# Splitting the last phase's weights ahead, handing the projection buffers over as rings, and a shrinking lead in the last unit of a streaming encoder layer

## The chip, the core and the metric

One core of a Trainium2 chip runs the whole layer as one program. The metric is the device time of one execution in microseconds (us), from the runs listed below. The core's engines work in parallel, each in the order of its own queue: PE (TensorE, matrix products and transposes; its weight loads are listed apart as PEld), DVE (VectorE), ACT (ScalarE), POOL (GpSimd), and SP, which issues the DMA transfers. They wait for each other through semaphores.

## What is computed

One layer over 2048 prompt rows (16 tiles of 128) and 8 x 16 sample rows (one more tile, called NT), model width 1024. Cut to its core:

```python
def adaln_modulate(x, c, norm_g, w_ada, b_ada):
    shift, scale, gate = jnp.split(c @ w_ada + b_ada, 3, axis=-1)
    return rms_norm(x, norm_g) * (1.0 + scale[:, None, :]) + shift[:, None, :], gate[:, None, :]

# qa ka va za (4 heads of 2 x 64), qb kb vb zb (8 heads of 64), gates ga gb: one product
qa, ka, va, za, qb, kb, vb, zb, ga, gb = jnp.split(h @ w_in, idx, axis=-1)   # rope on qa, ka

# a: softmax pair, mask by chunks of 64     w = p[0] - lam * p[1]
# b: stick breaking, mask kpos < qpos       log_a = log_sigmoid(z) + (suffix sum of log_sigmoid(-z))
oa, ob = diff_attention(qa, ka, va), stick_breaking_attention(qb, kb, vb)

oa = rms_norm(oa, subln_g) * (1.0 - lam_init)
ya = (oa * silu(za)) @ w_branch_a
yb = (ob * silu(zb)) @ w_branch_b
y  = x + gate * ((sigmoid(ga) * ya + sigmoid(gb) * yb) @ w_out)
return rms_norm(y, final_g)          # and the new keys and values
```

The sample rows attend to a cache of 512 positions per stream as well. Everything is float32 in and out; the products are made in pairs of float16 numbers.

## The kernel before

**Split numbers.** A float32 operand is scaled and written as a float16 high part and a float16 rest (`split`, L266: the high part on ACT, POOL or DVE, the rest on DVE by one scalar_tensor_tensor at L274). A product is then three float16 products. The scale comes from the sum of squares of the whole operand (`sum_squares` L246, `scales` L212), so weights are read once for their norm and once more to be cut.

**Phases.** First, adaLN and the modulated rows, written split to DRAM (`hT_d`). Then eight *units*, one for each of the four a-heads and four pairs of b-heads in turn (kind 0 and 1). A unit projects each of the 17 tiles (24 matmuls of 512 columns, L409), makes a slice of the gates for it as well (L476; none in the first unit, 512 columns wide in the last, 256 in the others), and runs attention for the 16 prompt tiles: scores (L611, L612), for kind 1 two sigmoids, a scan on DVE (L588) and a product on POOL (L594), then a cast and a subtraction (L544, L545), a DMA transpose (`wt`, L552), and two steps later the products with the values (`pv`, L663, L664). Results go to DRAM (`o_d`, `z_d`, `g_d`). The *last phase* reads them for each tile: `inputs` (L1105) normalises, applies silu and splits to u16, transposes it to uT; `branches` (L1218) multiplies by the branch weights `wb`, merges by the gates, splits to y16 and transposes to yT; `output` (L1253) multiplies by `wo` and writes the row. The sample's attention over the cache runs beside it, as 55 lists of pieces (`lane`, L1287) dealt to the tiles' iterations by `aside`.

**What sets the order.** The main loop (L1162) goes through the 136 steps (unit, tile). At each it takes pieces from one long line of projection pieces up to a target position and interleaves them with the step's scores and the products of two steps before. The target is the share of the attention time passed, plus `LEAD`, 5 tiles: projection stays five tiles ahead of attention. *Spare* work, one piece at a time, fills in after the next unit's weights are ready (L1174): 80 pieces that only sum squares, of the 16 slices of the branch and output weights and of 64 slices of the caches. When the line is at its end, `early_work` gives the freed projection memory to the last phase: it cuts the branch weights (8 pieces) and makes the inputs of the first two tiles. A scheduler then sorts the instructions of each engine by a model of readiness, so the order in which they are written is a wish.

**Memory.** The projection's buffers are pools on the right side: 12 pieces of split weights (`wpr`), two staging tiles (`wst`), three tiles of rows (`hst`, tag hg), six gate weights (`gw`) and two gate results (`gt`). `proj.close()` frees them all; then wb (4 MB), the inputs' tiles (`inp`) and a stage for cutting are opened there. The output weights are cut at the start of the last phase, in memory freed by attention (L1205), through two tiles that the output rows use later.

## Time and profile before

| | us |
|---|---|
| median of three runs | 2507.16 (2504.18 to 2513.22) |
| the profiled execution | 2508.37 |
| its span, first to last instruction | 2506.5 |
| last gate matmul of the units starts | 1850.44 |
| last product of attention with values starts | 1925.69 |
| first branch matmul starts | 1933.03 |
| first output matmul starts | 1960.8 |
| mean granted TensorE clock | 0.940 |

In a row of the page's instruction groups stand: line, engine, operation, output and inputs by the program's names (buffer numbers left out), shapes and count, then busy time and mean duration in ns, then the idle time of the engine before them and what ended it. In a row of waits: who waited for what, total us, times, longest. In a timeline row: start, duration, engine, line, and in brackets the idle time before and its releaser. The 40 digits of a slice row are tenths of the time that the engine was busy, for TensorE's clock (PEclk) tenths of full speed. A matmul's duration includes its passage through the array, so that neighbours overlap; the distance between starts is its price.

### The profile page before, as it was taken

The numbers are of one execution on the slowest core, as the hardware profiler recorded it, in microseconds if no ns is written. First come the engines' busy times: TensorE is split into PE (matmuls) and PEld (weight loads), VectorE is DVE, ScalarE is ACT, GpSimd is POOL, SyncE is SP. The second block draws the span as 40 slices with busy tenths as digits, with TensorE's granted clock in tenths as the row PEclk, the third lists the DMA queues.
The fourth block names the chain that finished last, engine by engine and source line by source line (L and its number), as shares of the span: only waits on it lengthen the run. The fifth ranks groups of instructions, "written<-read, shape, count | busy, mean of one in ns | idle before, by whom it ended". The sixth has DMA issues, their size and how long they took to land. (4 is left out here: it accounts for less than half of the span.)

```text
span 2506.5 us, 45283 instructions
## 1 busy us (share of the span) xinstructions
PE 2195.5 (88%) x16366; PEld 1275.3 (51%) x16366; DVE 1793.3 (72%) x3762; ACT 1602.7 (64%) x3200; POOL 827.6 (33%) x671
## 2 busy tenths in 40 slices
PE   7859898899999988889989888999975788889997
PEld 3435555455655555556655555555543344444443
DVE  3577846877676678757577876656787888888765
ACT  2558757787767688657678876656775545445542
POOL 1543113354211244311034442102344454544422
PEclk8979999999999999999999999999985799899999
DMA  9578878998787899767679976656678989888531
GB/s 287 183 221 206 211 175 200 196 220 191 180 193 185 198 222 212 172 152 183 157 192 194 219 190 177 160 132 142 153 168 206 257 224 242 242 212 229 167 111 51
DMA packets 890994, 477.07 MB, mean 190 GB/s; under 512 B 540074, under 2 KB 842330, under 8 KB 890256
## 3 DMA queue, kind: packets, MB, share of 16 engines
q1 hardware_dynamic: 890768, 474.17, 76.6%
q8 instruction: 128, 2.10, 0.4%
q14 instruction: 98, 0.80, 0.1%
HBM read 272.94 MB, written 73.44 MB: 138 GB/s over the span
## 5 line engine op out<-in xcount | busy, mean ns | idle before, releaser
L409 PE MATMUL ps_mm<-wpair,hg 128*128 128x512 f16 x3120 | 789.7, 388 | 58.1 <-DMA hg<-hT_d 54.4
L594 POOL TENSOR_TENSOR sc_p<-sc_p,sc_n 128x127 f32<-128x127 f32 (+7 forms) x192 | 314.0, 1639 | 807.3 <-DVE sc_n L588 796.0
L409 PEld LDWEIGHTS <-hg 128*128 128x128 f16 x3120 | 281.9, 100 | 328.9 <-DMA hg<-hT_d 62.5
L476 PE MATMUL ps_t<-gw,hg 128*128 128x256 f16 (+1 forms) x2856 | 397.6, 293 | 2.3 <-DVE qst L504 2.3
L476 PEld LDWEIGHTS <-hg 128*128 128x128 f16 x2856 | 280.4, 100 | 96.0 <-DVE qst L504 2.6
L588 DVE TENSOR_TENSOR_SCAN sc_n<-ps_s,sc_n,zero_t 128x512 f32<-128x512 f32 x192 | 245.6, 1279 | 63.4 <-ACT ps_s L121 58.2
L611 PE MATMUL ps_s<-k,qst 128*128 128x512 f16 (+3 forms) x640 | 226.5, 355 | 53.3 <-DVE sc_n L588 41.2
L545 DVE TENSOR_TENSOR sc_n<-sc_p,sc_n 128x128 f16<-128x128 f32 (+7 forms) x192 | 229.7, 1201 | 39.2 <-ACT sc_n L544 38.8
L121 ACT ACTIVATE sc_p<-ps_s,usc 128x512 f32<-128x512 f32 (+3 forms) x320 | 205.0, 641 | 47.1 <-PE ps_s L612 25.6
L612 PE MATMUL ps_s<-k,qst 128*128 128x512 f16 (+3 forms) x640 | 226.3, 356 | 0.0
L1227 PE MATMUL ps_mm<-wb,uT 128*128 128x512 f16 x816 | 206.8, 407 | 20.5 <-DVE o L1125 12.5
L121 ACT ACTIVATE ps_s<-ps_s,usc 128x512 f32<-128x512 f32 (+3 forms) x328 | 199.9, 610 | 0.0
L1266 PE MATMUL ps_o<-wo,yT 128*128 128x512 f16 x816 | 193.0, 390 | 6.9 <-ACT wo L269 2.4
L663 PE MATMUL ps_o<-v,wt 128*128 128x128 f16 x1088 | 156.5, 226 | 39.8 <-DMA wt<-sc_n 39.7
L544 ACT CAST sc_n<-sc_p 128x128 f16<-128x128 f32 (+7 forms) x192 | 154.8, 813 | 49.5 <-POOL sc_p L594 48.7
L442 POOL TENSOR_TENSOR rot<-pr,rope 128x256 f32<-128x256 f32 x68 | 59.8, 879 | 351.8 <-ACT pr L423 293.7
L251 ACT ACTIVATE junk<-wst 128x1024 f16<-128x1024 f32 x124 | 131.6, 1062 | 47.2 <-DMA wst<-in_w_in_dram 17.4
L663 PEld LDWEIGHTS <-wt 128*128 128x128 f16 x1088 | 104.0, 102 | 90.3 <-DMA wt<-sc_n 49.7
L1227 PEld LDWEIGHTS <-uT 128*128 128x128 f16 x816 | 82.7, 104 | 125.3 <-issue 50.8
L530 DVE TENSOR_SCALAR_CACHE_REDUCE sc_n<-ps_s,usc 128x512 f32<-128x512 f32 (+3 forms) x160 | 106.6, 666 | 55.2 <-PE ps_s L615 34.2
L664 PE MATMUL ps_o<-v,wt 128*128 128x64 f16 x1088 | 145.2, 198 | 0.0
L530 DVE TENSOR_SCALAR_CACHE_REDUCE sc_p<-ps_s,usc 128x512 f32<-128x512 f32 (+3 forms) x160 | 106.5, 666 | 52.6 <-PE ps_s L612 41.7
(295 smaller groups left out, 4372.9 us busy)
## 6 DMA issues: line engine op xcount, KB each, us to landing
hg<-hT_d SPq DMA_DIRECT2D x130, 512.0 KB, 4.5
wst<-in_w_in_dram SPq DMA_DIRECT2D x112, 256.0 KB, 3.8
g<-g_d SPq DMA_DIRECT2D x34, 512.0 KB, 5.8
wst<-in_w_in_dram SPq DMA_DIRECT2D x32, 512.0 KB, 4.8
out_dram<-pr SPq DMA_DIRECT2D x204, 64.0 KB, 2.3
g_d<-gt SPq DMA_DIRECT2D x102, 128.0 KB, 3.1
wide<-in_w_ada_dram SPq DMA_DIRECT2D x12, 1024.0 KB, 10.3
z_d<-pr SPq DMA_DIRECT2D x136, 64.0 KB, 1.8
```

The lines of the kernel that those rows point to most:

```text
L121: i = S.activation(**kw)
L409: T.matmul(box["p"], box["h"][:, hi, k, :], U["w"][k][:, wi, :], start=(n == 0), stop=(n == 3 * KT - 1))
L476: T.matmul(box["g"][:, 0:gw], box["h"][:, hi, k, :], U["wg"][k // per][:, k % per, wi, :], start=(j == 0), stop=(j == 3 * KT - 1))
L530: V.tensor_scalar(out=dst[:, lo : lo + n], in0=p[:, 0:n], scalar1=sc_pos, scalar2=None, op0=ALU.mult, op1=ALU.max, accum_out=job["mx"][:, ...
L545: V.tensor_tensor(out=lo, in0=src, in1=hi, op=ALU.subtract)
L588: V.tensor_tensor_scan(out=dst[:, lo : lo + n][:, ::-1], data0=src[:, 0:n][:, ::-1], data1=zero_t[:, 0:1].to_broadcast([P, n]), initial=fi ...
L594: G.tensor_tensor(out=p[:, 0:m], in0=p[:, 0:m], in1=n[:, 1 : m + 1], op=ALU.mult)
L611: T.matmul(p[:, 0:n], qst[:, c, :], kk[:, c, 0:n], start=True, stop=False)
L612: T.matmul(p[:, 0:n], qst[:, 2 + c, :], kk[:, c, 0:n], start=False, stop=not diag)
L663: T.matmul(po[:, c * P : (c + 1) * P], wt[:, wj, :], vt[:, c, :, :], start=first, stop=False)
L1227: T.matmul(pb, st["u"][:, ui * 8 + br * 4 + k, :], wb[:, br, wi, k, c], start=(n == 0), stop=(n == 11))
L1266: T.matmul(po, st["y"][:, yi * 8 + k, :], wo[:, wi, k, c], start=(n == 0), stop=(n == 3 * KT - 1))
```

## The change

In words, part by part:

- *Weights.* The 16 cuts of the branch and output weights become 16 further pieces at the end of the spare work. Each loads 512 KB, splits it into one of two `cut` tiles, and stores the result to DRAM (`w2_d`). The spare work is dealt so that it ends with the seventh unit (before, it could reach into the eighth). The last phase loads the split pieces and cuts nothing.
- *Rings.* The projection's pools become lists of tiles of 4 KB a partition that are handed round by hand (`buf`). Six w tiles hold two split weight pieces each, as many as the twelve before; gt is one tile used in halves; two `cut` tiles are new. They stay open to the end: wb lies in two tiles each of cut, wst, w and gw, loaded as these come free from 15 steps before the end; o, z and u16 of the last phase lie in the three hg tiles, the gates in the other four gw tiles, uT in two w tiles, yT in the last two w tiles (one before), and y16 in the same tile as u16 (before: a tile of its own).
- *Lead.* In the last unit the target is written anew: from 5 tiles ahead at its start, the line's end is reached at 87% of the unit's time instead of about 70%.
- *First tiles.* After the line's end, seven pieces: inputs of two tiles, the four branch halves of the first tile with its finish, and the inputs of the third tile. The last phase's loop starts at 1; the lane of 55 lists is dealt to iterations 1 to 12 instead of 0 to 12.

The diff, cut where lines only moved or follow from those shown (`branches` moved out of the last phase into the layer's body, with the buffers named above):

```diff
-W_BUFS = 12
-G_BUFS = 6
+LAST = 0.87
+RINGS = {"w": 6, "wst": 2, "gw": 6, "hg": 3, "gt": 1, "cut": 2}
...
+    w2_d = [dram.tile([P, 2, 2, 512], F16, name=f"w2_d{i}") for i in range(16)]
-    proj = ctx.enter_context(ExitStack())
-    wpr = proj.enter_context(tc.tile_pool(name="wpr", bufs=W_BUFS, side="right", reuse_waits="tile"))
-    wst = proj.enter_context(tc.tile_pool(name="wst", bufs=2, side="right", reuse_waits="tile"))
+    rings, turns = {}, {}
+    def open_rings(name, tags):
+        pool = ctx.enter_context(tc.tile_pool(name=name, bufs=1, side="right", reuse_waits="tile"))
+        for tag in tags:
+            rings[tag] = [pool.tile([P, 1024], F32, name=f"{tag}{i}") for i in range(RINGS[tag])]
+            turns[tag] = 0
+    def buf(tag, dt=F32):
+        b = rings[tag][turns[tag] % len(rings[tag])]
+        turns[tag] += 1
+        return b if dt == F32 else b.bitcast(dt)
+    open_rings("ring0", ("w", "wst"))
...
-            st = wst.tile([P, 2, 4, P], F32, tag="wst", name="wst") if keep is None else keep[:, k // 2, :, :, :]
+            st = buf("wst").rearrange("p (k j n) -> p k j n", k=2, n=P) if keep is None else keep[:, k // 2, :, :, :]
...
-            w = gwp.tile([P, gk, 2, gw], F16, tag="gw", name="gw", bufs=G_BUFS)
+            w = buf("gw", F16).rearrange("p (k f n) -> p k f n", k=gk, f=2)
...
+            pair = buf("w", F16).rearrange("p (i f n) -> p i f n", i=2, f=2)
-                w = wpr.tile([P, 2, 512], F16, tag="wpair", name="wpair")
+                w = pair[:, i, :, :]
...
-        ahead[u, t] = hst.tile([P, 2, KT, P], F16, tag="hg", name="hg")
+        ahead[u, t] = buf("hg", F16).rearrange("p (f k n) -> p f k n", f=2, n=P)
...
-                gt = gwp.tile([P, 512], F32, tag="gt", name="gt", bufs=2)
+                gt = rings["gt"][0][:, t % 2 * 512 : t % 2 * 512 + 512]
...
-            st = wst.tile([P, 2, 4, P], F32, tag="wst", name="wst").rearrange("p k j n -> p (k j n)")
+            st = buf("wst")
-        return [lambda src=src, dst=dst: one(src, dst) for src, dst in srcs]
+        def cut(i):
+            if i == 0:
+                L["s"] = [scales(total(add_up(wsums[:, lo : lo + 8], 8)), con, f"s_w{lo}") for lo in (0, 8)]
+            src, k = ((w_ba, w_bb)[i // 4], i // 2 % 2 * 2) if i < 8 else (w_out, (i - 8) // 2 * 2)
+            st = buf("wst").rearrange("p (k n) -> p k n", k=2)
+            load(out=st, in_=src[:, k : k + 2, i % 2 * 512 : i % 2 * 512 + 512])
+            w = buf("cut", F16).rearrange("p (f k n) -> p f k n", f=2, k=2)
+            split(w[:, 0, :, :], w[:, 1, :, :], st, L["s"][i // 8][:, 0:1], S if i % 2 else G)
+            load(out=w2_d[i], in_=w)
+        return [lambda src=src, dst=dst: one(src, dst) for src, dst in srcs] + [lambda i=i: cut(i) for i in range(16)]
+    L = {}
...
-    hst = proj.enter_context(tc.tile_pool(name="hst", bufs=3, side="right", reuse_waits="tile"))
-    gwp = proj.enter_context(tc.tile_pool(name="gwp", bufs=1, side="right", reuse_waits="tile"))
+    open_rings("ring1", ("gw", "hg", "gt", "cut"))
-    late_weights = {}
-    cutting = ctx.enter_context(ExitStack())
-    L = {}
-    def cut(dst, src, k, j, s, n, pool, tag, bufs):
-        st = pool.tile([P, 2, 512], F32, tag=tag, name="wst2", bufs=bufs)
-        cols = slice(j * 512, (j + 1) * 512)
-        load(out=st, in_=src[:, k : k + 2, cols])
-        split(dst[:, 0, k : k + 2, cols], dst[:, 1, k : k + 2, cols], st, s[:, 0:1], S if n % 2 else G)
+    def weight(i, b):
+        b = b.rearrange("p (f k n) -> p f k n", f=2, k=2)
+        load(out=b, in_=w2_d[i])
+        return b
...
-        inp = L["inp"]
-        o = inp.tile([P, D], F32, tag="o2", name="o2")
+        o, z = rings["hg"][0], rings["hg"][1]
-        z = inp.tile([P, D], F32, tag="z2", name="z2")
-            gs.append(inp.tile([P, 2, 512], F32, tag="g2", name="g2", bufs=4))
+            gs.append(buf("gw").rearrange("p (b n) -> p b n", b=2))
...
-        u16 = inp.tile([P, 2, D], F16, tag="u16", name="u16")
+        u16 = rings["hg"][2].bitcast(F16).rearrange("p (f n) -> p f n", f=2)
-        uT = inp.tile([P, 16, P], F16, tag="uT", name="uT", bufs=2)
+        uT = buf("w", F16).rearrange("p (k n) -> p k n", n=P)
...
+    def branches(st):
...
+                    T.matmul(pb, st["u"][:, ui * 8 + br * 4 + k, :], L["wb"][br * 4 + k // 2 * 2 + j][:, wi, k % 2, :], start=(n == 0), stop=(n == 11))
...
+            y16 = rings["hg"][2].bitcast(F16).rearrange("p (f n) -> p f n", f=2)
...
+            yT = buf("y", F16).rearrange("p (k n) -> p k n", n=P)
...
-        res = ctx.enter_context(tc.tile_pool(name="resw", bufs=1, side="right", reuse_waits="tile"))
-        L["wb"] = res.tile([P, 2, 2, 4, D], F16, name="wb")
-        L["inp"] = ctx.enter_context(tc.tile_pool(name="inp", bufs=1, side="right", reuse_waits="tile"))
-        L["s"] = [scales(total(add_up(wsums[:, lo : lo + 8], 8)), con, f"s_w{lo}") for lo in (0, 8)]
-        stage = cutting.enter_context(tc.tile_pool(name="stage", bufs=1, side="right", reuse_waits="tile"))
-        made = [lambda k=k, j=j, br=br: cut(L["wb"][:, br, :, :, :], (w_ba, w_bb)[br], k, j, L["s"][0], br + k, stage, "wst2", 1)
-                for br in range(2) for k in (0, 2) for j in range(2)]
-        return made + [lambda t=t: first(t) for t in tiles[0:2]]
+        rings["w"] = [rings["w"][(turns["w"] + i) % 6] for i in range(4)]
+        rings["gw"] = [rings["gw"][(turns["gw"] + i) % 6] for i in range(4)]
+        turns["w"] = turns["gw"] = 0
+        rings["y"], turns["y"] = rings["w"][2:4], 0
+        del rings["w"][2:4]
+        def branch(j):
+            if j == 0:
+                L["b"] = branches(states[tiles[0]])
+            L["b"][j][1]()
+        return [lambda t=t: first(t) for t in tiles[0:2]] + [lambda j=j: branch(j) for j in range(4)] + [lambda: first(tiles[2])]
...
-                for _ in spare[: -(-len(spare) // ((NT + 1 - t % NT) + 8 * (6 - min(u, 6))))]:
+                for _ in spare[: -(-len(spare) // ((NT - t % NT) + 8 * (6 - min(u, 6))))]:
-        target = position(len(steps) * past / whole + LEAD)
+        target = len(steps) * past / whole + LEAD
+        if n >= 7 * (NT + 1):
+            target = 7 * (NT + 1) + LEAD + (NT + 1 - LEAD) / LAST * (8 * past / whole - 7)
+            if n >= len(steps) - 15 and not spare and len(L.setdefault("wb", [])) < 8:
+                i = len(L["wb"])
+                L["wb"].append(weight(i, buf(("cut", "wst", "w", "gw")[i // 2], F16)))
+        target = position(target)
-                proj.close()
-    cutting.close()
...
-        wb, (s_b, s_o) = L["wb"], L["s"]
-        wo = res.tile([P, 2, KT, D], F16, name="wo")
-        for n, (k, j) in enumerate((k, j) for j in range(2) for k in range(0, KT, 2)):
-            cut(wo, w_out, k, j, s_o, n, s2, "x", 2)
+        wo = [weight(8 + i, res.tile([P, 2048], F16, name=f"wo{i}")) for i in (0, 2, 4, 6, 1, 3, 5, 7)]
-        fg = res.tile([P, D], F32, name="fg")
+        fg = rings["gt"][0]
...
-                        T.matmul(po, st["y"][:, yi * 8 + k, :], wo[:, wi, k, c], start=(n == 0), stop=(n == 3 * KT - 1))
+                        T.matmul(po, st["y"][:, yi * 8 + k, :], wo[j * 4 + k // 2][:, wi, k % 2, :], start=(n == 0), stop=(n == 3 * KT - 1))
...
-        for n in range(NT + 2):
+        for n in range(1, NT + 2):
-            if n + 2 <= NT:
+            if 2 < n + 2 <= NT:
...
```

59 lines of the change are left out of this document (27 added, 32 removed).

## The prediction

> **What bounds the kernel now.** I read the page first, then the busy time by stretch, then the waits and the timeline of the worst stretch.
>
> ```profile
> span 2506.5 us, 45283 instructions
> PE 2195.5 (88%) x16366; PEld 1275.3 (51%) x16366; DVE 1793.3 (72%) x3762; ACT 1602.7 (64%) x3200; POOL 827.6 (33%) x671
> PE   7859898899999988889989888999975788889997
> DVE  3577846877676678757577876656787888888765
> PEclk8979999999999999999999999999985799899999
> DMA  9578878998787899767679976656678989888531
> ```
>
> PE carries the kernel, 88% of the span; only around slices 30 to 33 does it fall to 7, 5 and 7 tenths, and its granted clock falls with it. The next table cuts that place at its own borders (columns: stretch, its length, busy time and instructions of PE, PEld, DVE, ACT, POOL, then granted clock, DMA share, GB/s).
>
> ```profile
> 1500.00:1600.00 100.00, 91.74 (x672) 56.41 (x671) 65.72 (x177) 66.06 (x150) 23.71 (x26) 0.98 0.67 170
> 1600.00:1630.00 30.00, 26.93 (x220) 17.33 (x218) 22.46 (x55) 17.61 (x39) 3.87 (x4) 1.00 0.64 164
> 1690.00:1851.00 161.00, 161.00 (x1087) 84.85 (x1086) 116.64 (x187) 110.89 (x224) 50.53 (x35) 1.00 0.62 142
> 1851.00:1927.00 76.00, 39.56 (x363) 26.31 (x361) 66.59 (x85) 52.63 (x82) 39.45 (x20) 0.65 0.90 195
> 1927.00:2000.00 73.00, 51.95 (x234) 21.22 (x233) 57.80 (x96) 32.89 (x45) 34.79 (x24) 0.74 1.02 271
> 2050.00:2350.00 300.00, 261.85 (x2179) 136.01 (x2180) 257.21 (x526) 149.14 (x249) 141.61 (x103) 0.93 0.86 229
> 2350.00:2435.00 85.00, 79.36 (x582) 40.99 (x580) 56.38 (x166) 42.80 (x70) 28.74 (x21) 0.94 0.35 115
> ```
>
> From 1690 to 1851 PE never rests while DVE idles 44 us of 161; from 1851 to 1927 it is the other way round: DVE 88% busy, PE 52% at clock 0.65. From 1927 to 2000 neither is full. Weighted by clock, PE does 39.56 x 0.65 + 51.95 x 0.74 = 64 us of work in these 149 us: 85 us are lost, and that is the most this change could win. What separates the stretches:
>
> ```profile
> 1840.88 1.03 PE L409 MATMUL ps_mm<-wpair,hg 128*128 128x512 f16 x4
> 1841.74 0.22 PE L663 MATMUL ps_o<-v,wt 128*128 128x128 f16 x1
> 1850.44 0.60 PE L476 MATMUL ps_t<-gw,hg 128*128 128x512 f16 x2
> 1925.69 0.26 PE L664 MATMUL ps_o<-v,wt 128*128 128x64 f16 x1
> 1933.03 7.93 PE L1227 MATMUL ps_mm<-wb,uT 128*128 128x512 f16 x24 [7.07 <-DVE o L1125]
> 1999.76 1.32 ACT L269 ACTIVATE y<-g,sy 128x512 f16<-128x512 f32 x2
> ```
>
> The last projection (the gate matmul at 1850.44) comes 75 us before the last attention product (1925.69); until 1933 PE has scores and products alone. The y row at 1999.76 is the split of tile 1's merged branches; I use its start as the milestone "tile 1's branches done". Four matmuls of 512 columns take 0.86 us start to start (1840.88 to 1841.74), 0.42 ns a column. What PE waits for from 1850 to 2010:
>
> ```profile
> PE ps_s L611 <- DVE sc_n L588: 18.5, 14, 3.1
> PE ps_o L663 <- DMA wt<-sc_n: 15.3, 9, 6.5
> PE ps_mm L1227 <- DVE o L1125: 8.8, 3, 7.1
> ```
>
> So DVE sets the end there: its scans, the transposes that follow its subtractions, and its work on the first tiles' inputs.
>
> **The change part by part.** *Order in the last unit.* The lead over attention shrinks from 5 tiles to none at 87% of the unit, so projection work goes later and attention earlier. Counted in the changed program's order on PE, 16 instead of 24 chunks of 512 score columns follow the last gate matmul, and from the unit's first projection to that matmul 580 thousand columns instead of 573 thousand stand in front of it: 7 thousand x 0.42 ns = 3 us, so it ends at about 1854. Its cover is unchanged: PE is full there, and DVE has the 44 idle us for the eight chunks that move in. After it, PE now also has both first tiles' branches (84 of 96 of those matmuls before the last product) instead of none.
>
> What DVE must do from 1854 to the milestone comes from this view of 1850 to 2010 (line, engine, form, count | busy us, mean ns | idle before):
>
> ```profile
> L588 DVE TENSOR_TENSOR_SCAN sc_n<-ps_s,sc_n,zero_t 128x512 f32<-128x512 f32 x19 | 24.3, 1279 | 1.6 <-ACT ps_s L121 0.8
> L545 DVE TENSOR_TENSOR sc_n<-sc_p,sc_n 128x1024 f16<-128x1024 f32 (+2 forms) x13 | 18.3, 1405 | 0.0
> L274 DVE SCALAR_TENSOR_TENSOR wb<-wst,s_w,wb 128x1024 f16<-128x1024 f32 x8 | 11.9, 1493 | 7.4 <-ACT wb L269 6.2 <-POOL wb L271 1.0
> L274 DVE SCALAR_TENSOR_TENSOR wo<-wst,s_w,wo 128x1024 f16<-128x1024 f32 x8 | 11.8, 1480 | 1.4 <-POOL wo L271 1.2 <-ACT wo L269 0.2
> L1119 DVE SCALAR_TENSOR_TENSOR o<-o,orms,g 128x128 f32<-128x128 f32 x16 | 10.0, 677 | 0.0
> L1229 DVE SCALAR_TENSOR_TENSOR g<-ps_mm,iu,g 128x512 f32<-128x512 f32 x10 | 7.4, 742 | 0.0
> L588 DVE TENSOR_TENSOR_SCAN sc_n<-ps_s,zero_t 128x256 f32<-128x256 f32 (+2 forms) x6 | 5.7, 946 | 0.0
> L274 DVE SCALAR_TENSOR_TENSOR u<-o,su,u 128x1024 f16<-128x1024 f32 x4 | 5.6, 1410 | 0.6 <-ACT u L269 0.6
> L1103 ACT COPY uT<-ps_s 128x1024 f16<-128x1024 f16 x6 | 5.8, 1006 | 1.3 <-PE ps_s L1102 1.3
> L1125 DVE TENSOR_TENSOR o<-o,ps_mm 128x512 f32<-128x512 f32 x8 | 5.3, 674 | 0.1
> L274 DVE SCALAR_TENSOR_TENSOR y<-g,sy,y 128x512 f16<-128x512 f32 x4 | 3.9, 995 | 0.6 <-ACT y L269 0.6
> ```
>
> Attention: 25 scans and 13 subtractions took 24.3 + 5.7 + 18.3 = 48.3 us, 1.93 a chunk; 16 chunks: 31. Inputs of three tiles, each 4 x 0.68 + 2 x 0.67 + 1.41 + about 1 of one-column steps = 6.5: 19.5. Eight branch products x 0.74: 6. Four y splits: 4, with 2 of small steps around them. Together 62.5 us. From 1851 to 2000 DVE was busy 124.4 of 149 us, 83%; at that density 62.5 us need 75, and the milestone comes at 1854 + 75 = 1929 instead of 2000: **-71**. On PE the same stretch holds 92 thousand columns, 39 us at full clock, so DVE stays the bound.
>
> *Weights split early.* The 8 wb and 8 wo splits (23.7 us of DVE) leave this place; they are not in the 62.5. In their place 16 such splits run as spare work, twelve of them from about 6.7 units of projections on, that is in the stretch 1500 to 1630. There DVE has 42 idle us and PE 11; the other half of each split goes to POOL and ACT in turn, both emptier than PE. The price lies between 0 (hidden) and 12 x 1.49 = 18 us (if DVE set the pace), and four more elsewhere. PE is the fuller one, so near the low end: **+5**.
>
> *Transfers.* 16 more stores of 512 KB, the 16 loads moved ahead, eight wb reloads at the start of the last unit; the eight wo reloads take the place of as many loads. SP issues in order, and each store waits there for its split with whatever stands behind it: the transposes (wt) that the products wait for, the hT loads (hg) that projections wait for. What such waits cost SP from 1100 to 1630, and how long the loads take (median us, last number):
>
> ```profile
> SPq L552 <- DVE sc_n L545: 29.6, 14, 5.4
> SPq L386 <- PE ps_t L476: 25.1, 12, 5.3
> hg<-hT_d SPq DMA_DIRECT2D x130, 512.0 KB, 4.5
> wst<-in_w_out_dram SPq DMA_DIRECT2D x16, 512.0 KB, 5.5
> ```
>
> A held issue is 2.1 us here (29.6 / 14). Bounds: 0, since hg and wt are issued ahead, to 40 issues x 2.1 = 84. With PE at 92 to 100% busy under the same queue today, nearly all is covered: **+6**. The reloads fall where DMA has a third of its time free.
>
> *Shared buffers.* u16 and y16 now are one buffer, so in each iteration the u split on ACT waits until PE has transposed y, where both stood back to back. u is needed only two iterations later, so 0 at best; at worst the wait is a copy of transposed columns (L1103, 1.01) plus a DVE split (1.41), 2.4 us in 15 iterations, 36. Behind the waiting split on ACT stand the next tile's sigmoids and the sample's casts, and PE's u transposes wait for it. ACT is half idle there (149 of 300) and PE has output matmuls to run: **+5**. Rings for wpair, gw, hg, wst keep their counts, and gt keeps two halves: 0 (a stall would show as hg or gt waits).
>
> *Sample work.* It starts one iteration later: its 55 steps (eight heads' 13 steps, started six apart) go over 12 iterations instead of 13, and five steps that lay before the milestone come after it. The tiles' period with and without it:
>
> ```profile
> L269 ACT ACTIVATE y<-g,sy x20: 704/706/721, 2049.8 to 2352.8; 128x512 f16<-128x512 f32 x20
> L269 ACT ACTIVATE y<-g,sy x8: 706/707/722, 2352.2 to 2434.6; 128x512 f16<-128x512 f32 x8
> ```
>
> Ten tiles' y in the first row, nine periods up to 2352.2: 33.6 us; then three periods of 27.2. The difference, 6.4, pays four to five steps, 1.45 each: five cost **+7**. Bounds: 0 to 16 (all at DVE's price: seven k16c splits and the like, at 86% busy).
>
> The sum: -71 + 5 + 6 + 5 + 7 = -48, against the profiled execution's 2508.37 us (span 2506.5 and 1.9 around it): **2460**. That execution lies 1.2 us above the median of 2507.16.
>
> **A rule that speaks against it.** The granted clock is 0.65 in the hole though its longest scan wait is 3.1 us. The Trainium skill ("TensorE: Matmul & The Clock Gate", section on the HAM clock gate) says that PE falls to half rate after an idle window of about 3.4 us and returns after as long a busy one. The trace agrees in kind, but the clock here fell among shorter gaps too. By that rule the filled tail, still DVE-bound with such gaps, would run its matmuls at half rate.
>
> **The rivals.**
> - *The forecast*, 0.55, with its own range 2440 to 2480.
> - *The sample work sets the last phase*, 0.20. Its tiles live in memory freed by attention, so it starts with the end of attention; if its chain (DMA share 1.02 and 0.86, DVE 257 of 300) sets the pace to the last tiles, only the earlier end of attention counts: the last product comes at 1854 + (31 + 13 for two tiles' inputs) / 0.88 = 1904 instead of 1926, -22, plus 5 and 6 of the early splits: 2498. For it: those shares. Against it: without sample work the period still is 27.2.
> - *SP's queue*, 0.10, the slower side. Each of the 40 added or moved issues holds transposes or hg back while PE runs dry. At 2.1 us each: 2460 - 6 + 84 = 2538. It decides from (48 + 6) / 40 = 1.35 us each. For it: the two SP rows. Against it: the 64 cache loads of the same size already run as spare work, with PE above 90% in 1500 to 1600.
> - *The one buffer for u and y* costs its full 36: 2491, 0.07. For it: fixed order on three engines. Against it: two iterations of slack.
> - *Half clock in the tail*, 0.05. 92 thousand columns at 0.84 ns are 77 us, 2 more than DVE's 75, and where the two don't overlap some 8 more (the first inputs' chain, as the 7 us wait of L1227 shows): 2470. For it: 0.65 from 1851 to 1927. Against it: PE then is asked for 39 us in 75 at full clock, twice as densely as the 26 in 76 now.
> - *Nothing moves*, 0.03: the scheduler sorts by readiness, and PE stays dry after 1854: 2508. For it: readiness, not the written order, decides. Against it: the count of 16 chunks instead of 24 is of the sorted program.
>
> **How the numbers follow.** Likeliest: 2460. Below: the iteration after the milestone took 50 us before instead of 33.6; if that goes too and the three +5s and 6s are nothing, 2460 - 16 - 16 = 2428; I end at 2432. Above: the second rival and half its scatter, 2506. Outside lie mainly SP's queue and little at the low end. 0.3% is 7.5 us and about what can be told apart. Faster by more: the forecast, half clock, most of the sample and buffer cases: 0.79. Within: the rest of these and "nothing moves": 0.08. Slower: the queue and an addition of smaller costs: 0.13.
>
> **What would show it.** Right: the last gate matmul near 1854; between it and the last product a granted clock above 0.8 and branch matmuls; no wb or wo splits; tile 1's y near 1929, then a period of about 34. Wrong: PE idle before 1630 behind hg or wt with SP waiting for splits (queue); u splits behind y's transposes with PE idle (buffer); a period near 36 or more (sample); the hole merely later. The forecast falls if the milestone gains 71 us and the end does not, or if unit 6 ends over 15 us late.

## The result, and the profile after

| | before | after |
|---|---|---|
| median, us | 2508.27 (2504.18 to 2513.22, 4 runs) | 2530.99 (2527.26 to 2532.19, 4 runs) |
| ratio | | 1.0098 (95%: 1.0077 to 1.0118) |
| profiled execution, its span | 2508.37, 2506.5 | 2532.19, 2530.4 |
| seventh unit starts, eighth unit starts | 1404, 1624 | 1412, 1652 |
| merge of tile 1, of tile 10 (its start on POOL) | 1988, 2308 | 1979, 2336 |

The kernel became about 23 us slower; 2460 was forecast, with 2506 as the upper end. A unit's start here is the first query row of its first tile on DVE, a merge the start of its second half on POOL. The first rows of the page of after:

```profile
span 2530.4 us, 45304 instructions
PE 2191.5 (87%) x16366; PEld 1271.9 (50%) x16366; DVE 1781.6 (70%) x3762; ACT 1600.7 (63%) x3200; POOL 829.1 (33%) x671
PE   7869888899998988899988889899996878878897
PEclk8979999999999999999999999999997989889899
DMA  9578878897788899667789987875576898888531
```

PE still carries the kernel, with as many instructions as before. The 7, 5, 7 of slices 30 to 32 became 9, 6, 8, so the hole did shrink; but PE shows 8 and its clock 8 in slices that had 9. The four rows of the timeline that answer to the prediction's milestones (last gate matmul, last product, first branch matmul, split of tile 1's merged branches):

```profile
1896.70 0.60 PE L492 MATMUL ps_t<-gw,hg 128*128 128x512 f16 x2
1975.24 0.19 PE L680 MATMUL ps_o<-v,wt 128*128 128x64 f16 x1
1943.33 1.01 PE L1172 MATMUL ps_mm<-cut,w 128*128 128x512 f16 x2 [5.37 <-DVE hg L1145]
1984.67 1.34 ACT L284 ACTIVATE hg<-gw,sy 128x512 f16<-128x512 f32 x2 [1.11 <-DVE sy L239]
```

Branch matmuls now run before the last product, as written (84 of the first two tiles' 96, the number forecast). But that product comes 50 us later than before (1975 against 1926), and the sample work, whose memory attention holds, starts later with it: the first cache load is issued at 1930.8 before and at 1990.1 after. From the last gate matmul to tile 1's split it takes 88 us instead of 149. The gate matmul comes 46 us later, and behind the split stand 546 us instead of 507 (2530.4 - 1984.7 against 2506.5 - 1999.8). 46 - 61 + 39 = +24.

The busy time by stretch, cut at these borders: seventh unit, eighth unit (to the last query row on DVE, called the last projection below; the gate matmuls of the changed kernel run on to 1897), transition (to the merge of tile 1), tiles 1 to 10, the rest. Before:

```profile
1404.00:1624.00 220.00, 197.74 (x1560) 124.76 (x1559) 158.43 (x349) 156.49 (x335) 73.25 (x66) 0.98 0.76 185
1624.00:1851.00 227.00, 227.00 (x1523) 120.22 (x1522) 154.59 (x279) 147.23 (x294) 50.53 (x35) 1.00 0.60 138
1851.00:1988.00 137.00, 83.11 (x578) 44.99 (x576) 113.46 (x159) 78.16 (x115) 66.48 (x40) 0.70 0.96 236
1988.00:2308.00 320.00, 276.07 (x2269) 141.05 (x2268) 272.96 (x556) 157.69 (x265) 157.00 (x111) 0.91 0.88 229
2308.00:2502.00 194.00, 173.27 (x1179) 86.77 (x1177) 127.90 (x329) 86.67 (x141) 62.61 (x47) 0.95 0.37 115
```

After:

```profile
1412.00:1652.00 240.00, 205.68 (x1538) 128.10 (x1536) 181.57 (x374) 155.28 (x328) 86.80 (x72) 0.94 0.87 226
1652.00:1887.00 235.00, 225.95 (x1592) 121.72 (x1590) 151.05 (x275) 145.09 (x291) 51.52 (x36) 1.00 0.65 146
1887.00:1979.00 92.00, 63.09 (x451) 36.02 (x450) 73.06 (x111) 62.91 (x98) 36.66 (x23) 0.78 0.68 164
1979.00:2336.00 357.00, 293.26 (x2362) 148.06 (x2362) 284.40 (x581) 163.49 (x271) 170.04 (x119) 0.88 0.89 239
2336.00:2525.00 189.00, 166.57 (x1156) 83.02 (x1154) 121.55 (x323) 84.31 (x138) 61.93 (x46) 0.95 0.37 115
```

The columns to read are the length, PE's and DVE's busy time, and the last three (clock, DMA share, GB/s). The seventh unit is 20 us longer with hardly other work on PE: 8 of it is PE's busy time at a lower clock, 12 are waits (22.3 and 34.0 us, summed over the rows of its waits). The eighth is 8 us longer, and PE, which never rested in it before, now has idle time. The transition is 45 us shorter. Tiles 1 to 10 are 37 us longer. And the DMA share changed sides: 0.96 to 0.68 in the transition, 0.76 to 0.87 in the seventh unit.

Borders like these shift when work is reordered, so a second reading checks them. Both kernels stream the same 4,967,448 columns of matmuls, a float32 column counted as four. The lag is how much later than the kernel before a kernel has done the same share of them, worked out from the matmuls' starts in the traces, at seven moments of the kernel before (us; 1474 is a third into the seventh unit, behind four of the cuts and ahead of the other twelve, 1648 and 1753 are in the eighth unit, 1866 is past the last projection, 2058 in the first tiles, 2494 at the last matmul):

```
                        1474   1648   1753   1866   2058   2250   2494
after                   +3.3  +26.7  +26.7  +35.6   -3.4  +26.2  +23.5
e2_two_cuts             -5.1   -9.2   +0.2  +11.8  -20.0  +14.9  +10.7
e3_no_split             +6.9  +25.6  +25.6  +33.9   -5.4  +20.0   +9.8
e4_no_store             -2.3  +15.2  +15.6  +13.7  -28.7   -0.1  -11.9
e13_loads_only          +5.8  +15.7  +15.8  +24.8  -15.1  +15.2  +15.8
e9_cuts_first          +36.6  +41.9  +41.9  +40.0   -0.5  +26.0  +17.3
e5_lead                 -4.9   -3.7   -3.7   +5.8   +7.6   +3.1   +4.8
e7_lane1                -0.9   -0.1   -0.1   +0.3  -13.2   +4.9   +8.6
e8_y_in_g               +5.9  +29.1  +29.1  +38.4   +0.6  +30.2  +21.3
e14_lane0               +7.0  +30.8  +30.8  +39.7  +35.0  +32.1  +39.7
e16_before_half_caches  +2.3   +0.7   +0.7   +1.1   -0.6   -2.1   -3.7
e17_after_half_caches   +3.6  +24.8  +24.8  +33.5   -3.4   -1.2   -1.1
```

For the changed kernel: 23 us lost in the stretch of the cuts, 9 in the eighth unit, 39 won in the transition, 27 given back while tiles 1 to 10 run. The other rows belong to the experiments; they are single profiles, and a few us between two rows mean nothing.

### The profile page after: what moved, and what is told of

Its sections match the earlier page's. It is cut to its first block, busy times and chain, and to the rows that moved or that the text cites. A ratio compares the mean times of both kernels' runs of the same rounds, so it can differ in the third digit from the quotient of the medians.

```text
span 2530.4 us, 45304 instructions
## 1 busy us (share of the span) xinstructions
PE 2191.5 (87%) x16366; PEld 1271.9 (50%) x16366; DVE 1781.6 (70%) x3762; ACT 1600.7 (63%) x3200; POOL 829.1 (33%) x671
## 5 line engine op out<-in xcount | busy, mean ns | idle before, releaser
L425 PE MATMUL ps_mm<-w,hg 128*128 128x512 f16 x3120 | 783.2, 389 | 85.3 <-DMA hg<-hT_d 78.3
L610 POOL TENSOR_TENSOR sc_p<-sc_p,sc_n 128x127 f32<-128x127 f32 (+7 forms) x192 | 307.5, 1605 | 797.3 <-DVE sc_n L604 776.9
L561 DVE TENSOR_TENSOR sc_n<-sc_p,sc_n 128x128 f16<-128x128 f32 (+7 forms) x192 | 221.2, 1156 | 44.3 <-ACT sc_n L560 43.6
L1290 PE MATMUL ps_o<-wo,w 128*128 128x512 f16 x816 | 192.6, 390 | 7.9 <-ACT w L1125 5.1
L679 PE MATMUL ps_o<-v,wt 128*128 128x128 f16 x1088 | 146.5, 226 | 37.2 <-DMA wt<-sc_n 36.7
L1172 PEld LDWEIGHTS <-w 128*128 128x128 f16 x816 | 81.8, 102 | 117.0 <-issue 38.0
L604 DVE TENSOR_TENSOR_SCAN sc_n<-ps_s,zero_t 128x128 f32<-128x128 f32 (+3 forms) x128 | 104.2, 815 | 45.7 <-ACT ps_s L123 42.7
L680 PE MATMUL ps_o<-v,wt 128*128 128x64 f16 x1088 | 136.3, 198 | 0.0
```

The source lines that it names most:

```text
L425: T.matmul(box["p"], box["h"][:, hi, k, :], U["w"][k][:, wi, :], start=(n == 0), stop=(n == 3 * KT - 1))
L561: V.tensor_tensor(out=lo, in0=src, in1=hi, op=ALU.subtract)
L604: V.tensor_tensor_scan(out=dst[:, lo : lo + n][:, ::-1], data0=src[:, 0:n][:, ::-1], data1=zero_t[:, 0:1].to_broadcast([P, n]), initial=fi ...
L610: G.tensor_tensor(out=p[:, 0:m], in0=p[:, 0:m], in1=n[:, 1 : m + 1], op=ALU.mult)
L679: T.matmul(po[:, c * P : (c + 1) * P], wt[:, wj, :], vt[:, c, :, :], start=first, stop=False)
L1290: T.matmul(po, st["y"][:, yi * 8 + k, :], wo[j * 4 + k // 2][:, wi, k % 2, :], start=(n == 0), stop=(n == 3 * KT - 1))
```

## The experiments

**The early cuts.** Three edits of the changed kernel leave out, for 14 of the 16 cuts, everything, the splits alone, or the stores alone; the last phase then reads the two remaining weights in place of all.

```diff
# e2_two_cuts
-        ... + [lambda i=i: cut(i) for i in range(16)]
+        ... + [lambda i=i: cut(i) for i in (0, 8)]
# e3_no_split, in cut(i), after the load
+            if i % 8:
+                load(out=w3_d[i], in_=st)
+                return
# e4_no_store, at the end of cut(i)
-            load(out=w2_d[i], in_=w)
+            if i % 8 == 0:
+                load(out=w2_d[i], in_=w)
```

> The changed kernel with 14 of the 16 early cuts left out (all weight tiles of the last phase are read from the two pieces that are still made, so the output isn't the reference's). Theory 'the cuts cost the units': the seventh unit, 220 us before and 240 with the change, comes back to 220 to 224, the sixth to 222, so the last unit starts at 1624 to 1630 instead of 1652, and the time falls by 20 to 28 us. Rival 'the rings themselves': the seventh unit stays above 235.

> The changed kernel with the 16 cuts kept as transfers: each loads its 512 KB and stores as many bytes, but 14 of them are not split (the last phase's weights are read from the two split pieces, so the output isn't the reference's). Theory 'engine work': the splits on DVE, ACT and POOL are what lengthens the seventh unit, so it comes down from 240 us to 220 to 226 and the last unit starts at 1622 to 1632, as with two cuts alone (1621). Rival 'transfers and SP's queue': it stays at 234 or more, the start at 1645 or later.

> The changed kernel with all 16 cuts made, but 14 of them not stored (the last phase's weights are read from the two stored pieces, so the output isn't the reference's). Theory 'engine work': the seventh unit stays at 234 us or more, the last unit's start at 1645 or later. Rival 'transfers and SP's queue': the stores that wait in SP's queue for their splits are the cost, and the unit comes down to 220 to 226, the start to 1622 to 1632.

Measured: 2520.98 (ratio 1.0054, 1.0031 to 1.0078), 2521.19 (1.0051, 1.0034 to 1.0068) and 2511.99 (1.0010, 0.9992 to 1.0028; its profiled execution, 2496.28, lies far below its median, so of e4 only the early columns of the lag are used). Without the cuts the eighth unit starts at 1621, no later than before; without the splits it starts at 1652, without the stores at 1642, so neither alone holds the units' loss. The total answers less than was expected of it: e2 is 10 us below the changed kernel and not 20 to 28, for its lag falls to -20 at 2058 and it gives back 31 us behind, so that it still ends above the kernel before. And e4, which leaves out only the stores, ends 9 us below e2, which leaves them out as well; that stays unexplained. The loads were left to be measured by themselves:

```diff
# e13_loads_only, in cut(i), after the load
+            if i % 8:
+                return
```

> The changed kernel with the sixteen early cuts reduced to their loads: for fourteen of them the weights are loaded into the staging tiles and neither split nor stored, and the last phase reads the two that are made in place of the others (the output is not the reference's). At equal TensorE work, against the kernel before, the seventh unit's lag grew by 24 us in the changed kernel, by 20 without the splits, by 14 to 17 without the stores, and fell by 8 with neither loads, splits nor stores. Theory A (additive: loads 18 to 22, splits 3 to 4, stores 7 to 10): with loads alone the lag grows by 10 to 14 us. Theory B (the loads by themselves are what the sums over the caches were before, 512 KB each, and cost little; it is their pile-up with splits and stores): it grows by under 5 us.

Measured: 2524.2 in one run. The seventh units of the four, from start to start of the eighth (two cuts, no splits, no stores, loads only):

```profile
1410.00:1621.00 211.00, 193.38 (x1553) 122.56 (x1553) 151.99 (x352) 150.10 (x324) 67.15 (x63) 1.00 0.77 185
```

```profile
1414.00:1652.00 238.00, 202.08 (x1573) 127.00 (x1571) 162.13 (x361) 150.43 (x323) 73.75 (x66) 0.96 0.90 228
```

```profile
1407.00:1642.00 235.00, 203.43 (x1558) 127.81 (x1557) 173.10 (x373) 155.71 (x329) 81.85 (x72) 0.96 0.84 207
```

```profile
1416.00:1645.00 229.00, 202.42 (x1589) 128.06 (x1588) 160.36 (x361) 149.51 (x323) 75.08 (x66) 0.98 0.88 214
```

From 1474 to 1648 the lag grows by 23.4 in the changed kernel, 18.7 without splits, 17.4 without stores, 9.9 with loads alone, and falls by 4.1 with two cuts. Counted from the last: loads 14, splits with loads 21.5, stores with loads 23, all three 27.5. That adds up within the scatter (14 + 7.5 + 9 = 30.5), so about three quarters of the price are transfers: the rows without splits have DVE near its old busy time and still 0.88 and 0.90 of DMA.

Most of it doesn't fall where the cuts run, though. Between 1474 and 1500 of the kernel before, the changed kernel's lag goes from 3.3 to 18.0; in its own time this is 1477 to 1518, while the fourth of its cuts is split at 1449 and the fifth at 1551. The stretch of equal work before and after:

```profile
1474.00:1500.00 26.00, 26.00 (x201) 16.19 (x200) 16.34 (x59) 20.50 (x53) 8.56 (x11) 1.00 0.79 214
```

```profile
1477.00:1518.00 41.00, 31.86 (x205) 18.27 (x204) 19.60 (x65) 26.88 (x65) 9.70 (x11) 0.88 0.92 228
```

What is loaded in it after is the last unit's weights, eight of 256 KB and six of 512 KB; the kernel before has only five of the large ones there, and had loaded the small ones by 1430, as e2 had, which loses nothing in this stretch. So a good part of the price may be that the first cuts pushed those loads onto one another. No run isolates that, and e9 below loses 10 us at the same place with its cuts long done.

Is it the place? In the next one the 16 cuts follow right after the weight sums, in the second and third unit:

```diff
# e9_cuts_first
-        return [... for src, dst in srcs] + [lambda i=i: cut(i) for i in range(16)]
+        made = [... for src, dst in srcs]
+        return made[0:16] + [lambda i=i: cut(i) for i in range(16)] + made[16:]
```

> The changed kernel with the sixteen early cuts done right after the sixteen weight sums, in the first units, instead of last in the list, which put them into the seventh unit. Theory A (a cut costs the loops some 1.7 us of transfers and of VectorE work wherever it runs: the seventh unit grew by 20 us and gave back 27 to 29 us when fourteen cuts were left out): the seventh unit goes back to about 220 us, but the units that take the cuts grow together by 15 to 25 us, so the last unit starts at about 1645 to 1655 as in the changed kernel and the time is 2522 to 2535. Theory B (it is the place: in the seventh unit the cuts stand between the last unit's weights in the staging ring and on the queues): the seventh unit is about 220 us and no other unit grows by over 5 us, the last unit starts at about 1630 and the time is 2505 to 2513.

Measured: 2522.8 (1.0064, 1.0042 to 1.0085). The second unit takes 259 us instead of 215, and at 1474 the lag is 37 us, to which the seventh unit adds 5: theory A, in that early cuts cost there too, and more (37 us, where 15 to 25 were expected). By its borders the seventh unit still takes 235 us and the last starts at 1681, which neither theory had; at equal work only those 5 us of it are left.

**Lead and buffers.** The lead alone and the shared buffer alone, put into the kernel before; and the sharing undone in the changed kernel, with y16 in halves of the gate tiles that the merge leaves free:

```diff
# e5_lead (kernel before)
-        target = position(len(steps) * past / whole + LEAD)
+        target = len(steps) * past / whole + LEAD
+        if n >= 7 * (NT + 1):
+            target = 7 * (NT + 1) + LEAD + (NT + 1 - LEAD) / LAST * (8 * past / whole - 7)
+        target = position(target)
# e6_share_y (kernel before)
-                y16 = s2.tile([P, 2, D], F16, tag="y16", name="y16", bufs=1)
+                y16 = L["inp"].tile([P, 2, D], F16, tag="u16", name="u16")
# e8_y_in_g (changed kernel)
-            y16 = rings["hg"][2].bitcast(F16).rearrange("p (f n) -> p f n", f=2)
+            y16 = [st["g"][j][:, 0, :].bitcast(F16).rearrange("p (f n) -> p f n", f=2) for j in range(2)]
```

> The kernel before with the new target in the last unit alone (87%). Theory 'the order in the last unit gains little by itself': the last projection moves from 1850 us to 1853 to 1862, attention ends 5 to 15 us earlier, and the time falls by 0 to 12 us from 2508. Rival 'it is most of the gain in the hole': tile 1's merge comes 25 us or more before 1988 and the time falls by 20 or more.

> The kernel before, with one change: y16 takes the buffer of u16. Theory 'one buffer': tile 1's merge to tile 10's goes from 320 us to 340 to 355, the time up by 20 to 35 us from 2508. Rival 'sample work later': up by at most 7 us.

> The changed kernel, but y16 lies in the halves of the gate tiles that are free after the merge, so u16 and y16 share nothing; uT and yT keep their two tiles each. Theory 'one buffer for u and y': tile 1's merge to tile 10's falls from 357 us to 335 or less, and the time by 15 us or more from 2531. Rival 'sample work later, and little else' (sharing alone added 4 us to that stretch in the kernel before): it falls by at most 10 us, the time by at most 10.

Measured: 2514.54 (1.0023, 1.0009 to 1.0038), 2513.31 (1.0011, 0.9992 to 1.0029) and 2530.27 (1.0088, 1.0061 to 1.0116). The lead by itself costs, where both theories had a gain: its lag grows by 9.5 us between 1753 and 1866, as the changed kernel's does (8.9), and its transition wins nothing. PE, which waited for nothing in the eighth unit before, now waits for rows of hT there, in the changed kernel and in e5:

```profile
PE ps_mm L425 <- DMA hg<-hT_d: 7.8, 6, 2.1
```

```profile
PE ps_mm L410 <- DMA hg<-hT_d: 7.8, 5, 2.2
```

The lead does not bring this wait by itself: e9 and e4 have the same target and no such row in that unit, and e9's lag doesn't grow there. What decides it was not found. The sharing is worth little either way: e8 takes the changed kernel's time, and e6 can't be told from the kernel before. A first try at it, e1_own_y, gave y16 one of the two yT tiles:

```diff
# e1_own_y (changed kernel)
-            y16 = rings["hg"][2].bitcast(F16).rearrange("p (f n) -> p f n", f=2)
+            y16 = rings["y16"][0].bitcast(F16).rearrange("p (f n) -> p f n", f=2)
-        rings["y"], turns["y"] = rings["w"][2:4], 0
+        rings["y"], turns["y"] = rings["w"][2:3], 0
+        rings["y16"] = rings["w"][3:4]
```

> The changed kernel, but y16 has a tile of its own again and yT one tile instead of two, as before the change. Theory 'one buffer for u and y': the stretch from tile 1's merge to tile 10's, 320 us before and 357 us with the change, comes back to 320 to 335, and the time falls by 20 to 35 us, to about 2500. Rival 'sample work one iteration later': that stretch stays at 350 or more and the time within 7 us of 2531. Both expect the units as with the change (the last unit's first tile at 1652 us).

Measured: 2583.48 (1.0304, 1.0271 to 1.0337). With one yT, a tile's transposes write over the tile before ahead of its output matmuls: another chain and other outputs, so it answers nothing about the sharing.

**The sample work.** One iteration later in the kernel before, nothing else:

```diff
# e7_lane1 (kernel before)
-            interleave(work, aside(n))
+            interleave(work, aside(n) if n else [])
```

> The kernel before, with one change: the sample's 55 lists are dealt to the tiles' iterations 1 to 12 instead of 0 to 12. Theory 'one buffer': the time rises by at most 7 us (the price that the prediction gave it). Rival 'sample work later': tile 1 to tile 10 goes from 320 to 340 or more and the time rises by 15 to 35 us, since fetches, key transposes and the tiles' inputs then collide.

Measured: 2517.27 (1.0042, 1.0023 to 1.0061): about +10, where the prediction had +7. It is made of two larger numbers: tile 1's merge comes 14 us earlier and tiles 1 to 10 take 343 us instead of 320. Then both kernels without this work:

```diff
# e11_before_no_sample, e12_after_no_sample
-        load(out=o, in_=o_d[t])
+        load(out=o, in_=o_d[t % NT])
-            interleave(work, aside(n))
+            interleave(work)
```

> The kernel before without the sample rows' attention in the last phase (none of its pieces is issued; the one token tile of the samples takes the first tile's attention values, so the sample outputs are not the reference's). With its partner for the changed kernel it asks what the 45 us were worth by which the transition got shorter. In both kernels TensorE waited 110 us in all between the last projection and the end. Theory A (the sample work filled the hole of the transition, so a shorter hole only moves that work and its waits on): without the sample work the two kernels differ, from last projection to last row, by far more than the 13 us that they differ with it, by 35 to 55 us. Theory B (the waits behind the transition come from the last phase's own chain, tile by tile, whatever the sample work does): they differ by 5 to 20 us. For this kernel by itself: last projection near 1850; the tile 1 merge at 1975 to 1990 in both theories (in A the hole stays, only emptier); from tile 1 to tile 10 some 200 to 240 us instead of 320.

> The changed kernel without the sample rows' attention in the last phase (left out as in its partner, with the same stand-in for the samples' token tile). Theory A: last projection to last row 35 to 55 us shorter than in the partner, nearly all of it before the merge of tile 1, and tile 1 to tile 10 within 8 us of the partner's. Theory B: 5 to 20 us shorter, and tile 1 to tile 10 longer than the partner's by 20 us or more, as with the sample work.

Measured: 2386.0 and 2377.62, one run each. Transition and tiles 1 to 10, kernel before without the samples, then changed kernel without them:

```profile
1843.00:1958.00 115.00, 68.67 (x512) 38.77 (x511) 99.70 (x139) 76.55 (x115) 56.97 (x31) 0.73 0.84 213
1958.00:2201.00 243.00, 218.65 (x1184) 104.42 (x1183) 154.87 (x403) 119.67 (x176) 71.87 (x57) 0.97 0.35 120
```

```profile
1880.00:1974.00 94.00, 63.61 (x464) 36.04 (x461) 73.25 (x110) 64.29 (x100) 35.68 (x21) 0.76 0.67 155
1974.00:2202.00 228.00, 213.85 (x1186) 103.58 (x1185) 146.42 (x405) 120.12 (x178) 76.88 (x58) 0.99 0.44 150
```

From last projection to last row: 536 and 491 us, 45 us apart, where with the samples it is 652 and 639, 13 apart (from the last gate matmul instead, 58 and 22). So the change does win its 45 us there, and the sample work, which costs 116 us before and 148 after, takes 32 back. Theory A in the total, not in the place: only 21 us of it lie before tile 1, 15 in tiles 1 to 10, the rest behind. On DVE the transition is 100 us before and 73 after, the cuts that are gone.

What the samples cost more of can be seen in the transfers. Transition, before (issues; the dc rows are the caches):

```profile
DMA packets 57065, 32.28 MB, mean 234 GB/s; under 512 B 39329, under 2 KB 49876, under 8 KB 57056
dc<-in_cache_a_k_dram SPq DMA_DIRECT2D x4, 512.0 KB, 4.4
dc<-in_cache_a_v_dram SPq DMA_DIRECT2D x4, 512.0 KB
dc<-in_cache_b_k_dram SPq DMA_DIRECT2D x3, 512.0 KB
```

Tiles 1 to 10, before; then the transition after, whose issues have no dc row; then tiles 1 to 10 after, with what PE waits for there:

```profile
DMA packets 128905, 73.14 MB, mean 229 GB/s; under 512 B 67480, under 2 KB 118885, under 8 KB 128875
```

```profile
DMA packets 30526, 15.20 MB, mean 163 GB/s; under 512 B 27133, under 2 KB 27645, under 8 KB 30519
```

```profile
DMA packets 149352, 85.48 MB, mean 239 GB/s; under 512 B 76657, under 2 KB 137969, under 8 KB 149321
PE ps_s L751 <- DMA dks<-k16c: 16.9, 5, 5.7
PE ps_t L782 <- DMA dwt<-dsc: 7.4, 4, 2.4
```

Eleven cache loads ran in the old transition, none in the new one (32.28 and 15.20 MB); the stretch behind it moves 12 MB more, and its DMA share was 0.88 already. PE's waits on DMA there, summed over all rows of the view, rise from 5.2 to 27.1 us; PE's busy time rises by 17 (276.07 to 293.26). 22 + 17 is the 37 us and 2 over. The busy time is in good part order: the stretch holds 52 thousand columns more, 26 thousand of them output matmuls of the first tile, of which the kernel before did a part ahead of tile 1's merge, and 17 thousand of the samples. L751 multiplies the cache keys that the dks transposes deliver. Is it the bytes? Both kernels with every second cache load left out (the tile loaded before it is used twice):

```diff
# e16_before_half_caches, e17_after_half_caches
-            box[name, i] = kc = dec.tile([P, 8, P], F32, tag="dc", name="dc", bufs=3)
+            if i % 2:
+                box[name, i] = box["c", name]
+                return
+            box[name, i] = box["c", name] = kc = dec.tile([P, 8, P], F32, tag="dc", name="dc", bufs=3)
```

> The kernel before with every second load of the sample caches in the last phase left out (the tile loaded before it is used twice, so the sample outputs are not the reference's; some 16 MB less are moved and no instruction on an engine is left out). Theory A (the last phase is bound by transfers as long as the sample work runs): tile 1 to tile 10 moves about 50 to 55 MB and takes 255 to 290 us instead of 320. Theory B (it is bound by the engines' work for the samples, the share of the transfers only goes along): 310 to 325 us.

> The changed kernel with the same loads left out. Theory A: tile 1 to tile 10 takes 265 to 300 us instead of 357, and from the last projection to the last row it is 25 to 45 us shorter than its partner, instead of 13. Theory B: 340 us or more, and 8 to 18 us shorter than its partner.

Measured: 2504.73 and 2507.28, one run each. Tiles 1 to 10 of the first and of the second:

```profile
1978.00:2303.00 325.00, 279.53 (x2297) 143.16 (x2295) 273.33 (x560) 158.90 (x265) 166.19 (x112) 0.91 0.73 189
```

```profile
1977.00:2314.00 337.00, 290.83 (x2344) 147.45 (x2344) 289.35 (x579) 163.38 (x271) 180.40 (x119) 0.89 0.80 209
```

Theory B holds for the kernel before: 12 MB less in this stretch, and it stays at 325 us (320). The changed kernel falls from 357 to 337, between the two theories, PE's waits on DMA from 27.1 to 8.3, and from last projection to last row it is 31 us shorter than its partner (616 against 647) instead of 13. In the lag, what it gives back from 2058 on falls from 27 to 5 us (2 of its own, and its partner wins 3). So before, the stretch was bound by the engines and had just room enough for the transfers; after, it is bound by both, and about 21 of the 27 us go with these loads (one run of each kernel).

The last two put the first sample lists ahead of the loop, so that they might fill the transition:

```diff
# e14_lane0 (changed kernel), e15_lane0_first (e9_cuts_first)
+        interleave(aside(0))
         for n in range(1, NT + 2):
```

> The changed kernel with the first of the sample lists issued ahead of the loop of the last phase, so that this work stands in the transition again, and the rest dealt over the same tiles as before. Theory A (the sample work lost its place in the transition and was paid for later): from the merge of tile 1 to that of tile 10 it takes 325 to 343 us instead of 357, tile 1 comes up to 15 us later than 1979, and the time is 2515 to 2525. Theory B (the sample work costs more room wherever it is): tile 1 to tile 10 gets no shorter than tile 1 gets later, and the time is 2528 to 2535.

> The changed kernel with both: the early cuts right after the weight sums, and the first of the sample lists ahead of the loop. Theory A: 2522.8 less what e14_lane0 gains, so 2507 to 2517. Theory B: as with the cuts moved alone, 2519 to 2527.

Measured: 2551.29 (1.0163, 1.0137 to 1.0188) and 2552.93 (1.0161, 1.0138 to 1.0184). Misses: tile 1's merge stays at 1983, and that of tile 2 moves from 2015 to 2061. The lists ran behind tile 1 as a block, with nothing beside them. Their tiles live in memory that attention holds until its last product (1980 in e14, its first cache load at 1994), so no list can start much before it; and tiles 1 to 10 took 360 us. A placement that helps was not found, and no version that does all the work beats the kernel before.

## Why the prediction failed

Beside the forecast's own milestones, with its +5 and +6 counted ahead of the gate matmul, the profiled execution is about 32 us late at that matmul (1865 forecast, 1897 measured), 13 us in the transition (75 and 88), and 28 us from tile 1's split to the end (518 and 546).

- *Weights split early*, predicted at +5 with bounds 0 to 18: 23 us. The step that failed is "PE is the fuller one, so near the low end", taken together with a bound that priced the splits alone. Splits were worth 5 to 8 us (e3 against the changed kernel, e4 against e13), as the bound allowed; the transfers of the same pieces, put into another term at +6 for 40 issues, made the rest. Both terms together measured 23 against +11, inside the sum of their bounds. SP holding issues back, the mechanism given for the transfers, isn't what shows: SP's waits in all, summed over the seventh unit, went from 126.5 to 123.5 us. PE's waits there grew by 11.7 us in several rows. The largest is that for landing rows of hT, before and after:

```profile
PE ps_mm L409 <- DMA hg<-hT_d: 7.6, 7, 2.4
```

```profile
PE ps_mm L425 <- DMA hg<-hT_d: 11.3, 7, 3.1
```

That is 3.7 us of it; waits for DVE's scores grew by 3.0, for transposes by 1.4. The same pieces also cost in the early units (e9). Which of them starts the chain stays open.
- *Order in the last unit.* "Its cover is unchanged: PE is full there" failed as well: 9 us by the lag, shown by e5, where +3 stood, with PE waiting 7.8 us for rows of hT. The gate matmul that was the milestone comes 46 us late because of this, of the cuts, and of standing later in the order.
- *The transition* was sized nearly right: 75 us predicted from the last gate matmul to tile 1's split, 88 measured, 149 before.
- *From the milestone to the end.* This step failed too, the one by which the gain was lost. The sum gave the 74 us of the transition to the end and charged the sample work +7. The transition was not only waiting: 11 cache loads and their lists ran in it. The row with a DMA share of 1.02 from 1927 to 2000 stood in the prediction and was used for a rival only; the 0.86 of the stretch behind it left the moved transfers little room there (e17). The sample work cost 32 us more (e11, e12).
- *Sample work one iteration later*, +7: by itself about +10 (e7). The term came out near for no good reason: it is a 14 us gain ahead of tile 1's merge and a 23 us loss behind it, and the prediction had neither. Whether the gain is part of the transition's 61 us was not tested.
- *Shared buffers*, +5: not to be told from nothing (e6 at most 7 us above the kernel before by its interval, e8 the same as the changed kernel).
- *The rivals.* "The sample work sets the last phase" named the right cause. Its 2498 assumed that the units lose 11 and that attention ends 22 us earlier; the lag at the last projection is 36 us, and attention ended 50 us later. The slow rival had the right place, transfers in the units, and a carrier, SP's waits, that doesn't show. Both signs that the text named for its fall came: the seventh unit ended 28 us late, and a gain of the transition did not reach the end.
- *The clock.* Between the last gate matmul and the last product it was to be above 0.8; it was 0.74 (1897 to 1975; 0.65 before), and 0.78 over the whole transition, 0.70 before.

## What to carry to other kernels

A hole in the busiest engine's row isn't idle time if another resource is full in it: read the DMA share of the hole and of the stretch behind it, and count the bytes that the change moves from one to the other. Cost a step that is made early with its transfers, in the stretch where they land; here cuts cost about 2 us each in units whose engines seemed to have room (27 us for the 14 that e2 leaves out, 37 for the 16 of e9). When a stretch gets shorter, follow the total from one fixed point to the end, and take the suspected neighbour out of both kernels: 13 us became 45.

## What the runs showed of the hardware

The granted clock falls without an idle window of the engine. Its half-rate stretches in the transition of after last 6.8, 13.7, 10.2, 6.8 and 3.4 us, multiples of 3.4. The Trainium skill ("TensorE: Matmul & The Clock Gate", the section on the HAM clock gate) speaks of a free-running window of about 3.4 us, which agrees, and of an idle one as the cause of the half rate. In the kernel before, however, matmuls filled a median of 0.33 of the 3.4 us ahead of the 42 falls, up to 0.66, and the longest gap in them had a median of 2.2 us: a thinly filled window is enough.

How much a full DMA would move goes here with the size of its packets. In tiles 1 to 10 of after, half the packets are under 512 B (76657 of 149352), and 239 GB/s at a share of 0.89 would be 269 at a full one. Without the samples (e12, its tiles 1 to 10) it is 150 at 0.44, which would be 341 if the rate grew with the share, with 1058 of 11770 packets so small. The Trainium skill ("DMA: Bandwidth & Descriptors", Specifications) puts the least size for full rate at 512 B; the two rows agree with that in kind.
